# A kernel that orders its own instructions: new durations in the estimate behind the order

## The chip, the cores and the metric

The kernel runs on one core of a Trainium2 chip. The metric is device time in microseconds: the median of several executions of one build. The engines are TensorE (PE, with its weight loads PEld), VectorE (DVE), ScalarE (ACT), GpSimd (POOL) and SyncE (SP), which here only issues DMAs.

## The reference, cut to what matters

Two streams of 256 tokens, 1024 features each, pass two layers: stream 0 holds the latent tokens (h below), stream 1 the context (hc).

```python
def ffn_half_step(h, g, shift, scale, gate, w13, w2):
    return h + 0.5 * gate * swiglu(modulate(rms_norm(h, g), shift, scale), w13, w2)

def reference(x, c, ctx, c_ctx, w_ada, ...):
    h, hc = x, ctx
    for i in range(DEPTH):
        m = jnp.split((silu_c @ w_ada[i] + b_ada[i])[:, None, :], N_MOD, axis=-1)
        ...
        h = ffn_half_step(h, g_ffn1[i], m[0], m[1], m[2], w13_ffn1[i], w2_ffn1[i])
        hc = ffn_half_step(hc, g_ffn1[i], mc[0], mc[1], mc[2], w13_ffn1[i], w2_ffn1[i])
        n_lat = modulate(rms_norm(h, g_mix[i]), m[3], m[4])
        z = n_lat @ w_in[i]
        ...
        y = mix_heads(z, ...) @ w_out[i]
        h = h + m[5] * y
        h = ffn_half_step(h, g_ffn2[i], m[6], m[7], m[8], w13_ffn2[i], w2_ffn2[i])
        ...
    return rms_norm(h, g_final)
```

`mix_heads` is a Fourier mixer, a small attention, a gated mixer over chunks and a pooling mixer, side by side. In the last layer the context passes only the first half-step and the keys and values. The inner width of an FFN is 2816, in three parts of 8, 7 and 7 blocks of 128.

## The kernel before, in words

Features lie on the 128 partitions in eight channels, tokens along the free axis: 512 columns are both streams, 256 one of them. Every large product is made from three matmuls (`mm3`, lines 187 to 193): a weight tile of 128 x 1024 is loaded (tile stg), ScalarE rounds it (whi, line 156), VectorE takes the rest (wlo, line 164), and the activations are split in the same way (n, and ghi and glo inside an FFN). Five pairs whi and wlo are held; when a weight tile has been used (`done`), the next one is converted.

A normalisation at the end of a stage goes through these steps, for each stream: VectorE adds the last output to h (line 168), ScalarE squares it (sq, line 156), POOL adds the square to acc (line 464), two pairs of small matmuls against ones reduce acc (line 183), VectorE adds the epsilon (ss, line 173), POOL takes the power (rs, line 492), VectorE puts it on a diagonal (dg, line 164), a matmul broadcasts it, and `apply` makes for each channel nt (VectorE, line 168), the high part of n (ScalarE, line 156) and the low part of n (VectorE, line 168). The next stage's products begin with stream 0 (`gemm_start`): for each channel in turn the products of two weight tiles, then the same for two further tiles, and then stream 1. Meanwhile the last four outputs of the stage before were made for stream 0 first and for stream 1 after it (`final_half`), each with a product per inner block.

The order is not written out. While the program is built, the class `Weaver` keeps an estimated time: `W.t` for TensorE and `W.free` for the other engines. Each emitted instruction advances them by a cost. Tasks (a generator for each normalisation, conversion, evacuation, attention head and so on) say by `yield` at which estimated time they go on; after each product, `tick` runs those whose time has come, and what they emit stands in the queues at that place. Each engine then works through its queue in that order, and real waits come from semaphores alone. So a cost is never executed; it moves instructions past one another. A result counts as there 60 ns after its engine's estimated end:

```python
    def pe(self, cost, after=0.0):
        self.t = max(self.t, after) + cost
        end = self.t + 150.0
        self.tick()
        return end

    def on(self, engine, cost, after=0.0):
        start = max(self.free[engine], after, self.t)
        self.free[engine] = start + cost
        return start + cost + 60.0
```

Where a product needs a channel whose n has not been emitted, `W.until` runs tasks ahead, in the order of their times, until it has; TensorE's estimated time then jumps. The costs touched are those of ScalarE (`act`, line 155), VectorE (`vcost`, line 160, and `vstt`, line 167), the products (`mm3`, line 187; lines 1305 to 1308 and 1321 to 1324 in the mixing) and POOL (`square_in`, line 464, and `rstd_tail`, line 492). Loads are issued by SP from a fixed list (`loads`), each when the conversion that frees its buffer has been emitted.

Of the kernel before, what the change touches and what calls it, by code (L numbers as in the profile page):

```python
# [128 lines left out]
def block_kernel(ctx: ExitStack, tc: tile.TileContext, ins, out: bass.AP):  # L129
    nc = tc.nc  # L130
    W = Weaver()
# [23 lines left out]
    def act(o, i, func, after=0.0, n=None, **kw):  # L155
        nc.scalar.activation(o, i, func, **kw)  # L156
        n = n or int(np.prod(o.shape[1:]))
        return W.on("a", 190.0 + 0.833 * n, after)

    def vcost(o):  # L160
        return 70.0 + 1.04 * int(np.prod(o.shape[1:]))

    def vtt(o, a, b, op, after=0.0):
        nc.vector.tensor_tensor(out=o, in0=a, in1=b, op=op)  # L164
        return W.on("v", vcost(o), after)

    def vstt(o, a, s, b, op0, op1, after=0.0):
        nc.vector.scalar_tensor_tensor(out=o, in0=a, scalar=s, in1=b, op0=op0, op1=op1)  # L168
        return W.on("v", vcost(o), after)

    def vts(o, a, s1, op0, s2=None, op1=None, after=0.0):
        if op1 is None:
            nc.vector.tensor_scalar(out=o, in0=a, scalar1=s1, scalar2=None, op0=op0)
        else:
            nc.vector.tensor_scalar(out=o, in0=a, scalar1=s1, scalar2=s2, op0=op0, op1=op1)
        return W.on("v", vcost(o), after)
# [5 lines left out]
    def mm(o, l, r, first, last, after=0.0, skip=False):  # L182
        nc.tensor.matmul(o, l, r, start=first, stop=last, skip_group_check=skip)  # L183
        n = int(np.prod(r.shape[1:]))
        return W.pe(max(110.0, 1.68 * n), after)

    def mm3(o, wh, wl, xh, xl, first, last, after=0.0, skip=False):
        n = int(np.prod(xh.shape[1:]))
        c = max(109.0, 0.4235 * n)
        nc.tensor.matmul(o, wh, xh, start=first, stop=False, skip_group_check=skip)  # L190
        nc.tensor.matmul(o, wh, xl, start=False, stop=False, skip_group_check=skip)  # L191
        nc.tensor.matmul(o, wl, xh, start=False, stop=last, skip_group_check=skip)  # L192
        return W.pe(3 * c, after)
# [98 lines left out]
    def conv(i, j, hi, lo):  # L292
        n = loads[j][2]
        raw = stage[j][:, :n]
        yield act(hi[:, :n], raw, AF.Copy)
        ready_t[i] = vtt(lo[:, :n], raw, hi[:, :n].bitcast(F32), ALU.subtract)
        ready[i] = (hi[:, :n], lo[:, :n])
        use(j)
# [7 lines left out]
    def done(i):  # L306
        over.add(i)
        while finished[0] in over:
            i = finished[0]
            finished[0] += 1  # L310
            ready.pop(i)
            conv_upto(i + AHEAD)
# [60 lines left out]
    def gain_from(l, i, c0=0, c1=KC, n=2):  # L373

        m = mods[l][:, :n, (1, 4, 7)[i] * 8 + c0:(1, 4, 7)[i] * 8 + c1]
        vstt(gains[l][:, i, :n, c0:c1], m, 1.0,
             gains[l, "g"][:, i, None, c0:c1].to_broadcast([P, n, c1 - c0]), ALU.add, ALU.mult)
# [70 lines left out]
    def square_in(v, c):  # L448

        if v not in acc:  # L450
            acc[v] = tmp.tile([P, T], F32, name="acc%d" % v, tag="acc%d" % v, bufs=1)
            acc_n[v] = acc_i[v] = 0
        i = acc_i[v]
        acc_i[v] += 1
        if i == 0:
            t1 = act(acc[v], h[:, c, v], AF.Square)
        else:
            s = yield from SQ.get()
            t1 = act(s, h[:, c, v], AF.Square)
            if i == KC - 1 and last[0]:  # L460
                last_sq[v] = s
            else:
                yield t1
                nc.gpsimd.tensor_tensor(out=acc[v], in0=acc[v], in1=s, op=ALU.add)  # L464
                t1 = W.on("g", 640.0)
                SQ.put(s)
        acc_n[v] += 1
        acc_t[v] = t1
# [18 lines left out]
    def rstd_tail(ps, t1, nblk, n_feat):  # L487
        yield t1
        ss = tmp.tile([P, 4], F32, name="ss", tag="ss", bufs=8)
        t1 = vts(ss[:, :nblk], ps[:, :nblk], n_feat * EPS, ALU.add, after=t1)  # L490
        rs = tmp.tile([P, 4], F32, name="rs", tag="rs", bufs=8)
        nc.gpsimd.tensor_tensor(out=rs[:, :nblk], in0=ss[:, :nblk], in1=mhalf.to_broadcast([P, nblk]), op=ALU.pow)
        t1 = W.on("g", 380 + 165 * nblk, t1)
        yield t1
        dg = yield from DG.get()
        dv = dg[:, :P * nblk].rearrange("p (b q) -> p b q", b=nblk)
        t1 = vtt(dv, ident[:, None, :].to_broadcast([P, nblk, P]),
                 rs[:, :nblk, None].to_broadcast([P, nblk, P]), ALU.mult, t1)
        yield t1
        t1 = mm(ps[:, :P * nblk], ones, dg[:, :P * nblk], True, True, t1)  # L500
        DG.put(dg)
        yield t1
# [6 lines left out]
    def n_of(c, v):  # L509
        if v is None:  # L510
            a = nt_[c][:, :4 * T].rearrange("p (v x) -> p v x", v=2)
            return a[:, :, :T], a[:, :, T:]
        o = 2 * T * v
        return nt_[c][:, o:o + T], nt_[c][:, o + T:o + 2 * T]
# [16 lines left out]
    def raw_in(l, i, c):  # L531
        hi, lo = (t[:, :T] for t in raw_of(c))
        x, a = h[:, c, 0], gain_of(l, i, 0, c)
        yield act(hi, x, AF.Copy, scale=a)
        vstt(lo, x, a, hi.bitcast(F32), ALU.mult, ALU.subtract)
        raw_done.add(c)
# [36 lines left out]
    def wk(i, k, n=P):  # L573
        a, b = get(i)
        return a[:, k * n:(k + 1) * n], b[:, k * n:(k + 1) * n]

    def ps_new():
        W.until(lambda: MM.free)
        return MM.take()
# [5 lines left out]
    def gemm(i, vs, nk=KC, xs=None, ps=None, ok=None, raw=False):  # L585

        ps = ps or ps_new()
        v = None if len(vs) == 2 else vs[0]
        o = ps[:, :T + 2] if raw else cols(ps, vs)
        for k in range(nk):  # L590
            wh, wl = wk(i, k)
            if ok:
                W.until(lambda: ok(k))
            xh, xl = raw_of(k) if raw else (xs or n_of)(k, v)
            mm3(o, wh, wl, xh, xl, k == 0, k == nk - 1)
        return ps
# [332 lines left out]
    def mixing(l, tail):  # L929
# [4 lines left out]
        with ExitStack() as es:  # L934
# [350 lines left out]
            def ev(o, i, f, key):  # L1285
                t1 = act(o, i, f) if f else vcopy(o, i)
                MM.put(key[1])
                yield t1
                st[key[0]] += 1
# [9 lines left out]
            for b in blks:  # L1299
                ps = ps_new()  # L1300
                v, tk = b // 2, slice((b % 2) * P, (b % 2) * P + P)
                for kk in range(KC):
                    wh, wl = wk(i0 + 5 + kk // 4, kk % 4, T)
                    xh, xl = n_of(kk, v)
                    nc.tensor.matmul(ps[:, :T], xh[:, tk], wh, start=kk == 0, stop=False)  # L1305
                    nc.tensor.matmul(ps[:, :T], xh[:, tk], wl, start=False, stop=False)  # L1306
                    nc.tensor.matmul(ps[:, :T], xl[:, tk], wh, start=False, stop=kk == KC - 1)
                    W.pe(327.0)
                W.spawn(ev(vg[:, b], ps[:, :T], AF.Gelu_apprx_tanh, ("vg", ps)), W.t + 200.0)
            done(i0 + 5)  # L1310
            done(i0 + 6)
            for v in vs:
                pss = [ps_new() for _ in range(2)]
                halves_ = ((0,), (1,)) if v != vs[-1] else ((0, 1),)
                for bs_ in halves_:
                    for kk in range(KC):
                        wh, wl = wk(i0 + 7 + kk // 2, kk % 2, 512)
                        xh, xl = n_of(kk, v)
                        for b in bs_:
                            ps, tk = pss[b], slice(b * P, b * P + P)  # L1320
                            nc.tensor.matmul(ps, xh[:, tk], wh, start=kk == 0, stop=False)  # L1321
                            nc.tensor.matmul(ps, xh[:, tk], wl, start=False, stop=False)  # L1322
                            nc.tensor.matmul(ps, xl[:, tk], wh, start=False, stop=kk == KC - 1)  # L1323
                            W.pe(648.0)
                        if kk % 2 and v == vs[-1]:
                            done(i0 + 7 + kk // 2)
                    for b in bs_:
                        W.spawn(ev(FP[:, 2 * v + b], pss[b], None if b else AF.Copy, ("fp", pss[b])), W.t + 200.0)
                n_free.add(v)
# [35 lines left out]
    vts(gfin, gfin, 32.0, ALU.mult)  # L1365
    begin_mods(1)
    mixing(0, norm_next(0, 2))
    load_pk2(1)
    ffn(0, 2, [0, 1], norm_next(1, 0))
# [140 lines left out]
```

## Time and profile before

| | us |
|---|---|
| median of 3 runs (1602.47 to 1604.53) | 1602.86 |
| the profiled execution's own time | 1602.9 |
| its span, from the first to the last instruction | 1600.8 |
| TensorE busy in the span | 1569.0 |
| VectorE, ScalarE, POOL busy | 1016.2, 559.3, 94.8 |

Times in rows count from the start of the span. The span is read against the profiled execution's own time: 2.1 us lie around it. TensorE's matmuls are pipelined, so the recorded duration of one overlaps with the next one's; its pace is read from how many start in a stretch. Inside an FFN half-step the kernel streams weight tiles; the boundaries where one stage's normalisation leads into the next stage's products are at about 390, 555, 920 and 1290 us, the mixings at 412 to 555 and 1310 to 1400 us.

### The profile page before, as it was taken

The numbers are of one execution on the slowest core, as the hardware profiler recorded it, in microseconds if no ns is written. First come the engines' busy times: TensorE is split into PE (matmuls) and PEld (weight loads), VectorE is DVE, ScalarE is ACT, GpSimd is POOL, SyncE is SP. The second block draws the span as 40 slices with busy tenths as digits, with TensorE's granted clock in tenths as the row PEclk, the third lists the DMA queues.
The fourth block names the chain that finished last, engine by engine and source line by source line (L and its number), as shares of the span: only waits on it lengthen the run. The fifth ranks groups of instructions, "written<-read, shape, count | busy, mean of one in ns | idle before, by whom it ended". The sixth has DMA issues, their size and how long they took to land.

```text
span 1600.8 us, 22427 instructions
## 1 busy us (share of the span) xinstructions
PE 1569.0 (98%) x8868; PEld 1348.3 (84%) x8868; DVE 1016.2 (63%) x1718; ACT 559.3 (35%) x845; POOL 94.8 (6%) x93
## 2 busy tenths in 40 slices
PE   6999999999999999999999999999999999999997
PEld 4788888889967998888888898888888897899997
DVE  5478787878657466555563366786563367776674
ACT  3332231323435352223222243222222355554443
POOL 0000000004100310000000210000000121100001
PEclk9999999999999999999999999999999999999999
DMA  9456655664211144354352234566473223265551
GB/s 354 191 168 206 196 190 179 221 193 154 80 38 53 55 183 163 122 170 137 129 171 93 77 113 164 176 236 231 160 237 111 93 86 106 92 204 180 167 193 61
DMA packets 72056, 245.52 MB, mean 153 GB/s; under 512 B 8336, under 2 KB 10640, under 8 KB 71184
## 3 DMA queue, kind: packets, MB, share of 16 engines
q1 hardware_dynamic: 71664, 243.71, 45.0%
q8 instruction: 69, 1.13, 0.3%
q10 hardware_dynamic: 288, 0.39, 0.1%
q14 instruction: 35, 0.29, 0.1%
HBM read 243.03 MB, written 1.05 MB: 152 GB/s over the span
## 4 chain that ended last, share of the span: by engine, by line
PE 94%; DVE 3%; ACT 1%; issue 1%; POOL 0%; DMA 0%; SPq 0%; DVEq 0%; ACTq 0%; POOLq 0%
PE mm L191 28%; PE mm L190 28%; PE mm L192 28%; PE mm L183 5%; DVE wlo L164 1%; PE mm L1321 1%; PE mm L1323 1%; PE mm L1322 1%; PE mm L196 1%; DVE nt L168 1%; DVE n L168 1%; PE mm L400 1%; POOL acc L464 0%; PE mm L1305 0%; PE mm L1306 0%
## 5 line engine op out<-in xcount | busy, mean ns | idle before, releaser
L190 PE MATMUL mm<-n,whi 128*128 128x512 f32 (+2 forms) x1804 | 624.4, 346 | 3.1 <-ACT whi L156 3.1
L191 PE MATMUL mm<-n,whi 128*128 128x512 f32 (+2 forms) x1804 | 620.4, 344 | 4.1 <-DVE n L168 3.3
L192 PE MATMUL mm<-n,wlo 128*128 128x512 f32 (+2 forms) x1804 | 617.8, 342 | 0.5 <-DVE wlo L164 0.5
L156 ACT ACTIVATE whi<-stg 128x1024 fp32r<-128x1024 f32 (+1 forms) x310 | 318.2, 1032 | 447.8 <-PE mm L191 194.1
L164 DVE TENSOR_TENSOR wlo<-stg,whi 128x1024 fp32r<-128x1024 f32 (+1 forms) x310 | 374.5, 1211 | 92.8 <-ACT whi L156 92.5
L190 PEld LDWEIGHTS mm<-n,whi 128*128 128x128 f32 x1804 | 343.4, 190 | 46.6 <-issue 4.8
L191 PEld LDWEIGHTS mm<-n,whi 128*128 128x128 f32 x1804 | 343.2, 190 | 46.7 <-DVE n L168 6.9
L192 PEld LDWEIGHTS mm<-n,wlo 128*128 128x128 f32 x1804 | 343.7, 191 | 39.5 <-DVE wlo L164 1.0
L426 DVE SCALAR_TENSOR_TENSOR junk<-stg,sbc 128x1024 bf16<-128x1024 f32 x224 | 274.5, 1226 | 8.1 <-DMA stg<-in_w_ada 6.1
L190 PE MATMUL mm<-ghi,whi 128*128 128x512 f32 (+1 forms) x788 | 270.8, 344 | 0.0
L191 PE MATMUL mm<-glo,whi 128*128 128x512 f32 (+1 forms) x788 | 270.2, 343 | 0.0
L192 PE MATMUL mm<-ghi,wlo 128*128 128x512 f32 (+1 forms) x788 | 270.0, 343 | 0.0
L168 DVE SCALAR_TENSOR_TENSOR h<-mm,gates,h 128x256 f32<-128x256 f32 x168 | 75.6, 479 | 147.0 <-PE mm L192 146.8
L191 PEld LDWEIGHTS mm<-glo,whi 128*128 128x128 f32 x788 | 149.3, 189 | 17.7
L190 PEld LDWEIGHTS mm<-ghi,whi 128*128 128x128 f32 x788 | 149.3, 189 | 17.4
L192 PEld LDWEIGHTS mm<-ghi,wlo 128*128 128x128 f32 x788 | 149.3, 189 | 17.3
L464 POOL TENSOR_TENSOR acc<-acc,sq 128x256 f32<-128x256 f32 x68 | 71.2, 1054 | 1361.1 <-ACT sq L156 1184.6
L164 DVE TENSOR_TENSOR g<-mm,s 128x512 f32<-128x512 f32 x66 | 45.6, 691 | 167.1 <-PE mm L192 166.5
L156 ACT ACTIVATE ghi<-g 128x512 fp32r<-128x512 f32 (+1 forms) x88 | 50.9, 578 | 275.4 <-DVE g L164 261.8
L164 DVE TENSOR_TENSOR glo<-g,ghi 128x512 fp32r<-128x512 f32 (+1 forms) x88 | 54.5, 620 | 18.2 <-ACT ghi L156 18.2
L156 ACT ACTIVATE n<-nt,mods 128x256 fp32r<-128x256 f32 x80 | 39.7, 508 | 69.5 <-DVE nt L168 68.6
L156 ACT ACTIVATE sq<-h 128x256 f32<-128x256 f32 x70 | 28.6, 416 | 86.3 <-DVE h L168 86.1
(151 smaller groups left out, 798.0 us busy)
## 6 DMA issues: line engine op xcount, KB each, us to landing
stg<-in_w_ffn SPq DMA_DIRECT2D x208, 512.0 KB, 4.2
stg<-in_w_ada SPq DMA_DIRECT2D x128, 512.0 KB, 3.8
stg<-in_w_ffn SPq DMA_DIRECT2D x64, 448.0 KB, 3.1
stg<-in_w_in SPq DMA_DIRECT2D x22, 512.0 KB, 3.3
stg<-in_w_out SPq DMA_DIRECT2D x16, 512.0 KB, 3.3
sbc<-in_cb SPq DMA_DIRECT2D x3, 1024.0 KB, 7.0
pk<-in_pk SPq DMA_DIRECT2D x2, 1344.0 KB, 8.3
h<-in_xT SPq DMA_DIRECT2D x4, 512.0 KB, 6.0
```

Of the source, the lines that this page charges most:

```text
L156: nc.scalar.activation(o, i, func, **kw)
L164: nc.vector.tensor_tensor(out=o, in0=a, in1=b, op=op)
L168: nc.vector.scalar_tensor_tensor(out=o, in0=a, scalar=s, in1=b, op0=op0, op1=op1)
L183: nc.tensor.matmul(o, l, r, start=first, stop=last, skip_group_check=skip)
L190: nc.tensor.matmul(o, wh, xh, start=first, stop=False, skip_group_check=skip)
L191: nc.tensor.matmul(o, wh, xl, start=False, stop=False, skip_group_check=skip)
L192: nc.tensor.matmul(o, wl, xh, start=False, stop=last, skip_group_check=skip)
L196: nc.tensor.transpose(o, i, ident)
L400: nc.tensor.matmul(ps[32 * g:32 * g + 32, :P], sc[:, k], w[:, 128 * g:128 * g + 128], start=k == 0, stop=k == KC - 1)
L426: nc.vector.scalar_tensor_tensor(out=ada_tiles["junk"], in0=stage[j], scalar=1.0, in1=ada_tiles["s"][:, v], op0=ALU.mult, op1=ALU.mult, ac ...
L464: nc.gpsimd.tensor_tensor(out=acc[v], in0=acc[v], in1=s, op=ALU.add)
L1321: nc.tensor.matmul(ps, xh[:, tk], wh, start=kk == 0, stop=False)
```

## The change

Only numbers of the estimate change. ScalarE: 200 + 0.834 ns per element in place of 190 + 0.833, or 280 where a bias or a scale goes in. VectorE: 150 + 1.045 ns per element in place of 70 + 1.04, and 60 more for an instruction with three operands. A matmul of a product: 118 ns up to 258 columns and 0.4434 ns per column above, in place of 109 or 0.4235. POOL: 1050 in place of 640 for the sum, 300 + 330 per block in place of 380 + 165 for the power. The three matmuls of the mixing's transposed products: 354 in place of 327 and 681 in place of 648.

```diff
@@ -155,10 +155,10 @@
     def act(o, i, func, after=0.0, n=None, **kw):
         nc.scalar.activation(o, i, func, **kw)
         n = n or int(np.prod(o.shape[1:]))
-        return W.on("a", 190.0 + 0.833 * n, after)
+        return W.on("a", (280.0 if "bias" in kw or "scale" in kw else 200.0) + 0.834 * n, after)
 
     def vcost(o):
-        return 70.0 + 1.04 * int(np.prod(o.shape[1:]))
+        return 150.0 + 1.045 * int(np.prod(o.shape[1:]))
@@ -166,7 +166,7 @@
     def vstt(o, a, s, b, op0, op1, after=0.0):
         nc.vector.scalar_tensor_tensor(out=o, in0=a, scalar=s, in1=b, op0=op0, op1=op1)
-        return W.on("v", vcost(o), after)
+        return W.on("v", vcost(o) + 60.0, after)
@@ -186,7 +186,7 @@
     def mm3(o, wh, wl, xh, xl, first, last, after=0.0, skip=False):
         n = int(np.prod(xh.shape[1:]))
-        c = max(109.0, 0.4235 * n)
+        c = 118.0 if n <= 258 else 0.4434 * n
@@ -462,7 +462,7 @@
                 nc.gpsimd.tensor_tensor(out=acc[v], in0=acc[v], in1=s, op=ALU.add)
-                t1 = W.on("g", 640.0)
+                t1 = W.on("g", 1050.0)
@@ -490,7 +490,7 @@
         nc.gpsimd.tensor_tensor(out=rs[:, :nblk], in0=ss[:, :nblk], in1=mhalf.to_broadcast([P, nblk]), op=ALU.pow)
-        t1 = W.on("g", 380 + 165 * nblk, t1)
+        t1 = W.on("g", 300 + 330 * nblk, t1)
@@ -1305,7 +1305,7 @@
-                    W.pe(327.0)
+                    W.pe(354.0)
@@ -1321,7 +1321,7 @@
-                            W.pe(648.0)
+                            W.pe(681.0)
```

## Rows read from the trace of the kernel before

**Rows 1.** The page: busy time by engine, and the chain that ended last by engine.
```profile
PE 1569.0 (98%) x8868; PEld 1348.3 (84%) x8868; DVE 1016.2 (63%) x1718; ACT 559.3 (35%) x845; POOL 94.8 (6%) x93
...
PE 94%; DVE 3%; ACT 1%; issue 1%; POOL 0%; DMA 0%; SPq 0%; DVEq 0%; ACTq 0%; POOLq 0%
```

**Rows 2.** Busy time in five stretches: from:to, us, busy by engine, clock, DMA, GB/s.
```profile
390.00:412.00 22.00, 19.75 (x129) 18.27 (x128) 17.80 (x40) 9.96 (x18) 7.27 (x6) 0.84 0.29 96
555.00:575.00 20.00, 19.04 (x154) 18.51 (x153) 16.77 (x33) 9.31 (x17) 6.34 (x6) 1.00 0.47 176
920.00:945.00 25.00, 23.09 (x168) 21.72 (x167) 20.35 (x42) 12.66 (x23) 7.85 (x7) 0.93 0.25 85
1290.00:1310.00 20.00, 17.67 (x131) 16.16 (x132) 17.83 (x37) 10.98 (x19) 5.98 (x6) 1.00 0.32 106
1310.00:1400.00 90.00, 88.53 (x599) 73.90 (x598) 67.42 (x136) 51.68 (x108) 10.86 (x9) 1.00 0.29 98
```

**Rows 3.** The same view of two steady stretches inside FFN half-steps.
```profile
80.00:120.00 40.00, 40.00 (x178) 33.11 (x177) 30.38 (x44) 12.81 (x18) 0.00 (x0) 1.00 0.52 168
1440.00:1480.00 40.00, 40.00 (x334) 40.00 (x334) 25.20 (x39) 16.73 (x20) 0.00 (x0) 1.00 0.54 184
```

**Rows 4.** Waits of TensorE: us in total, times, longest us.
```profile
PE mm L183 <- POOL acc L464: 3.4, 4, 0.9
PE mm L191 <- DVE n L168: 3.3, 7, 0.7
...
PE mm L183 <- DVE es L164: 2.1, 2, 1.6
```

**Rows 5.** Groups of instructions by form: busy us, mean ns of one, idle before.
```profile
L164 DVE TENSOR_TENSOR wlo<-stg,whi 128x1024 fp32r<-128x1024 f32 x246 | 304.2, 1240 | 75.0 <-ACT whi L156 74.8
...
L464 POOL TENSOR_TENSOR acc<-acc,sq 128x256 f32<-128x256 f32 x68 | 71.2, 1054 | 1361.1 <-ACT sq L156 1184.6 <-issue 173.4 <-ACT n L156 2.9
```

**Rows 6.** VectorE's timeline at the first boundary: start us, duration us, instruction.
```profile
400.52 0.47 DVE L168 SCALAR_TENSOR_TENSOR h<-mm,gates,h 128x256 f32<-128x256 f32 x1
400.91 0.47 DVE L168 SCALAR_TENSOR_TENSOR n<-nt,mods,n 128x256 fp32r<-128x256 f32 x1
401.31 1.21 DVE L164 TENSOR_TENSOR wlo<-stg,whi 128x1024 fp32r<-128x1024 f32 x1
402.44 0.47 DVE L168 SCALAR_TENSOR_TENSOR nt<-h,gains,mm 128x256 f32<-128x256 f32 x1
```

**Rows 7.** POOL's timeline there, idle time before and its releaser in brackets.
```profile
388.45 0.74 POOL L464 TENSOR_TENSOR acc<-acc,sq 128x256 f32<-128x256 f32 x1 [1.78 <-ACT sq L156]
...
401.64 1.46 POOL L464 TENSOR_TENSOR acc<-acc,sq 128x256 f32<-128x256 f32 x1 [2.08 <-ACT sq L156]
```

**Rows 8.** TensorE's timeline: the reduction for stream 1 at 403 and 569 us.
```profile
403.16 0.92 PE L183 MATMUL mm<-ones,acc 128*128 128x1 f32 x4 [0.86 <-POOL acc L464]
...
569.58 0.61 PE L183 MATMUL mm<-ones,acc 128*128 128x1 f32 x4 [0.86 <-POOL acc L464]
```

**Rows 9.** VectorE's timeline at 934 us: the fourth channel's n, and ss.
```profile
934.05 0.55 DVE L168 SCALAR_TENSOR_TENSOR n<-nt,mods,n 128x256 fp32r<-128x256 f32 x1
935.02 0.16 DVE L173 TENSOR_SCALAR ss<-mm 128x2 f32<-128x2 f32 x1 [0.41 <-PE mm L183]
```

**Rows 10.** VectorE's timeline at 555 to 575 us: the fourth n, the last h.
```profile
565.67 0.96 DVE L168 SCALAR_TENSOR_TENSOR n<-nt,mods,n 128x256 fp32r<-128x256 f32 x1
...
566.96 0.46 DVE L168 SCALAR_TENSOR_TENSOR h<-mm,mods,h 128x256 f32<-128x256 f32 x1
```

**Rows 11.** Busy time and granted clock in three stretches after the reductions.
```profile
403.20:410.00 6.80, 6.58 (x26) 5.94 (x27) 4.10 (x11) 2.17 (x5) 0.88 (x1) 0.51 0.24 77
...
935.60:939.10 3.50, 3.41 (x17) 3.10 (x15) 2.27 (x6) 1.53 (x3) 0.36 (x1) 0.52 0.20 81
...
1303.80:1309.00 5.20, 4.81 (x35) 4.14 (x34) 4.61 (x13) 2.96 (x6) 0.48 (x1) 1.00 0.16 65
```

## The prediction

> **What bounds the kernel now.** I read the page first: TensorE is busy for 98% of the span and holds 94% of the chain that ended last [rows 1]. A new order of the same instructions can therefore win only what TensorE loses by waiting or by a low clock. The table of stretches tells where that is [rows 2, 3]: inside an FFN half-step TensorE is busy all the time; what is missing lies in the second mixing (1.5 of 90 us idle) and at four boundaries where a normalisation ends a stage: idle 2.3 us at 390, 1.0 us at 555, 1.9 us at 920 and 2.3 us at 1290. The waits name the cause [rows 4]: the reduction of the squares waits four times for POOL's last sum, 3.4 us in all, and products wait seven times for n, the low part of a channel from VectorE, 3.3 us. So the boundaries can give back at most about 7.5 us of idle time, and what the clock adds to that (below).
>
> **The pace of TensorE.** In steady stretches 178 matmuls of 512 columns pass in 40 us, or 334 of about 256 [rows 3]: 225 and 120 ns each. The new 227 and 118 say this; the old 217 and 109 were 4% and 9% too low. The products themselves stay as they are and cost nothing more: only their place in the estimate's time moves.
>
> **The pace of the other engines.** The new figures are the rows' durations: 1220 ns against 1240 for wlo, 1050 against 1054 for POOL's sum [rows 5], 477 ns against 0.47 us for h and nt [rows 6]. But the starts in a row show something else [rows 6]: h starts at 400.52 us, n at 400.91, wlo at 401.31, nt at 402.44. The next instruction starts 0.39 us after one that is recorded with 0.47, and 1.13 us after a wlo that is recorded with 1.21: VectorE is occupied for 0.08 us less than the duration. The old 1135 ns for wlo was nearer to this, the old 336 ns for h and nt 0.05 us short, the new 477 is 0.09 us long. The Trainium skill, page Perfetto Trace Analysis, section Optimizing Scalar/DVE Operations, speaks against the change in the same way: an instruction's profiled latency is longer than the engine's busy time, since the acknowledgement of the write overlaps with the next instruction. The trace agrees [rows 6]; by that rule alone the VectorE edits bring nothing, and the sum below would be 0.
>
> POOL's sum is not one number either: 0.74 us at 388.45, 1.46 us at 401.64 while wlo runs [rows 6, 7]. 1050 lies between the two; the last sum of a boundary, which TensorE waits for, is the long one. The Trainium skill, page SBUF — State Buffer, section SBUF: two separate sides, has the rule: GpSimd and a VectorE instruction with two SBUF inputs exclude each other for a whole instruction. The trace agrees with it [rows 6, 7]; by it no constant fits both cases. The remaining edits (ScalarE with a bias, rs, the mixing's products) move the estimate the same way and are in the counts that follow.
>
> **The change at a boundary, step by step.** A tick of the estimate is one product of three matmuls: 327 ns before, 354 after. From stream 0's last product on, the estimate has the update of h at tick 1, the square at 3, the sum at 5, and the reduction is due at 1635 + 640 + 60 = 2335 ns before and 1770 + 1050 + 60 = 2880 after: tick 8 before, 9 after, so one product (0.36 us) later. Then ss, rs and dg: with all costs put in, the broadcast matmul stays at tick 16 at the boundaries that an FFN ends, and goes from 14 to 16 at 555 us; a wlo holds VectorE there meanwhile, so I cost that at nothing (0.2 us if that cover is gone).
>
> Then the channels. `apply` resumes 336 + 60 - 100 = 296 ns after nt before, which is one tick, and after 300 ns more, one tick: a channel every 2 ticks (0.72 us of TensorE). After, 477 + 60 - 100 = 437 ns is over 354: two ticks, and then one: a channel every 3 ticks (1.08 us). VectorE itself needs 2 x 0.39 = 0.79 us. Stream 1's last four outputs take seven ticks each, and a weight tile and an h go with each: before, 2289 = 1135 + 336 + 672c gives c = 1.2 channels; after, 2478 = 1220 + 477 + 954c gives 0.8; the chip can do (2.52 - 1.13 - 0.39) / 0.79 = 1.3. Followed tick by tick, VectorE's order at 390, 920 and 1290 us stays the same up to the second channel's n. Then stream 1's last h goes ahead of the fourth nt, and the fourth tile's wlo, now behind the third n (401.31 after 400.91 [rows 6]), goes ahead of it. No wait is added, and no DMA changes its place: SP issues the loads from a fixed list.
>
> The bill, boundary by boundary:
> - At 390 us the third n starts 1.13 us later, about 402.05, and its two products end about 403.2. h and the square come 0.39 us earlier, so the sum is ready by then. Before, the reduction started at 403.16, after waiting [rows 8]. Cost 0.1 us: the wait moves from the sum to n.
> - At 920 and 1290 us it is the same, but there the fourth n stood ahead of ss (934.05 and 935.02 [rows 9]); now it stands behind, starts about 935.1 in place of 934.05 and is late for products that could start about 935.1 and need it complete (0.47 us): 0.4 us each.
> - At 555 us an output takes eight ticks, and four n were through before the last h (565.67 and 566.96 [rows 10]). With 3 ticks a channel two are through, and the fourth wlo stands ahead of the fourth n. Five channels' products ended with the reduction waiting 0.9 us until 569.58 [rows 8], so they began about 569.6 - 0.9 - 5 x 0.72 = 565.1. From there h, n, nt, wlo end at 565.1 + 3 x 0.39 + 1.13 = 567.4 at best, the fourth n with its 0.47 and the wait for whi about 568.2, when three channels' products have been over for 1 us; the fifth n stands behind ss and costs 0.6 us more (an estimate from the 0.92 and 0.61 us of the reductions, which ss waits for [rows 8]). That is 1.6 in place of 0.9: 0.7 us.
>
> Bounds where the trace has no such row: the second mixing and the start. There the other engines' figures grow together with TensorE's, and new waits cannot be read. The idle time there, 1.5 us in the mixing and 2.1 us for es at the start [rows 2, 4], is the most to be gained; I take the same amounts as the most to be lost, and the middle, 0, because neither end is nearer to a row. At the tail each step waits for the one before, whatever the estimate: 0.
>
> Sum: 0.1 + 0.7 + 0.4 + 0.4 = 1.6 us on the profiled execution's own 1602.9 us, which agrees with the median of the runs shown (1602.86): **1604.5 us**. About 0.2% (3.2 us) can be told from no change here, so the forecast is no change.
>
> **Rivals.** (A) Faster: the truer pace of TensorE and POOL puts the reductions behind ready sums, and the clock stays up. For it: there are four such waits [rows 4], and a low clock follows two of them, granted 0.51 (1.2 GHz instead of 2.4) from 403.2 to 410 and 0.52 from 935.6 to 939.1, while 1303.8 to 1309 had 1.00 [rows 11]. At the latter's rate 26 matmuls take 26/35 x 5.2 = 3.9 us, not 6.8, and 17 take 2.5, not 3.5: 3.9 us lost. With half of the 3.4 us this gives 1602.9 - 5.6 = 1597.3 us. Against it: VectorE is the engine that is late, and it does no less. Chance 0.23.
>
> (B) Slower: the clock falls at the other two boundaries as well. Before, a wait of TensorE at a boundary was at most 0.9 us long [rows 4]; with wlo ahead of the third n there is one of 1.5 to 2 us. It decides as soon as such a wait lowers the clock at 555 and 1290 us, which have 1.00 now [rows 2]. Price: the 1.6 us and twice the mean of 2.9 and 1.0 us: 1602.9 + 1.6 + 3.9 = 1608.4 us. Against it: at 1290 us 2.3 us of idle time left the clock at 1.00. Chance 0.30.
>
> (C) The change does not do what it says: all figures grow by similar shares, and what moves is hidden: 1602.9 us. For it: until the second n my count gives the very same order. Against it: 3 ticks in place of 2. Chance 0.17.
>
> **Numbers.** The forecast has 0.30; it and C are no change, 0.47; faster 0.23; slower 0.30. The forecast's own range is 1602.9 to 1606. From 1597 (A) to 1609 (B) some 0.18 is left out, stronger forms of A and B; the unknown 3.6 us of mixing and start lie inside.
>
> **What would show it.** Right: wlo ahead of the third n on VectorE near 401, 932 and 1301 us; waits for POOL's sum near 0 in the list, waits for n of 5 us or more; 178 and 334 matmuls in 40 us as before. A: the waits for n fall too, and no stretch has 0.5. B: a third and a fourth stretch at 0.5. Wrong altogether: a wait inside an FFN half-step, or a mixing longer by over 2 us; I foresee neither.

## The result and the profile after

The changed kernel takes 1622.14 us (median of four runs, 1621.01 to 1623.26) against 1603.55 for the kernel before (four runs, 1602.47 to 1604.53): a ratio of 1.0118, interval 1.0105 to 1.0130. It is slower by 18.6 us, where 1604.5 us and no change had been forecast; the forecast's own range ended at 1606 and that with the rivals at 1609. The profiled execution took 1621.01 us; its span is 1619.1 us, 18.3 more than before.

The page of the kernel after, busy time by engine and the chain by engine [rows 1]:

```profile
PE 1574.0 (97%) x8880; PEld 1352.0 (83%) x8880; DVE 1019.4 (63%) x1718; ACT 557.8 (34%) x845; POOL 97.1 (6%) x93
...
PE 93%; DVE 4%; issue 1%; ACT 1%; POOL 0%; DMA 0%; SPq 0%; DVEq 0%; ACTq 0%; POOLq 0%
```

The work is the same; VectorE still does 1718 instructions. Of the 18.3 us, 13.3 are idle time of TensorE (45.1 us in place of 31.8); the other 5.0 are more busy time, of which the lower clock told below is a part. The waits of TensorE after, in us in total, times and longest [rows 4], say what it waited for:

```profile
PE mm L191 <- DVE n L168: 10.4, 11, 2.2
PE mm L192 <- DVE wlo L164: 9.5, 4, 3.2
...
PE mm L183 <- POOL acc L464: 0.9, 1, 0.9
```

The wait for POOL's sum has shrunk as predicted, from 3.4 to 0.9 us (the one that is left is at the boundary of 555 us), and the wait for n has grown from 3.3 to 10.4. Products also wait 9.5 us for wlo, the low part of a weight tile. The same line before:

```profile
PE mm L192 <- DVE wlo L164: 0.5, 1, 0.5
```

Of the 9.5 us, 2.0 are at the start and 7.5, in three waits, inside the first FFN half-step. Steady stretches show it: one of before, then three of after (the table of stretches, columns as in [rows 2, 3]):

```profile
240.00:280.00 40.00, 40.00 (x178) 33.13 (x177) 31.65 (x55) 7.46 (x9) 0.00 (x0) 1.00 0.54 181
```

```profile
80.00:120.00 40.00, 40.00 (x178) 33.13 (x177) 29.51 (x42) 12.94 (x17) 0.00 (x0) 1.00 0.51 172
240.00:280.00 40.00, 37.34 (x165) 30.61 (x164) 29.83 (x50) 7.20 (x9) 0.00 (x0) 1.00 0.54 176
360.00:400.00 40.00, 35.19 (x194) 30.47 (x194) 26.47 (x41) 11.46 (x20) 12.26 (x10) 0.96 0.48 162
```

The first stretch after has the 178 matmuls of [rows 3]. The next two lie inside the first FFN half-step and lack 2.7 and 4.8 us of TensorE at a granted clock of 1.00 and 0.96: the place that the prediction had left out as full.

**A ledger by stage.** I divided both spans at the first weight load for a product on n or on ghi of each part and took the differences of the stage lengths. Every part of the other FFN half-steps is the same to 0.01 us, apart from the stretches where a half-step ends.

| stage | us more after |
|---|---|
| start, and the first part's first matrix | 0.9 |
| first half-step, 2nd matrix of the second part (243.5 to 281.6 before) | 2.95 |
| first half-step, last part (281.6 to 398.1 before) | 0.2 + 7.3 |
| from there through the first mixing to 655 us | 2.4 |
| end of the second half-step and boundary at 930 us | 0.35 + 1.05 |
| end of the third half-step, boundary at 1298 us and second mixing | 0.35 + 2.8 |
| sum | 18.3 |

So 10.5 us are lost in the first half-step, some 7 at the boundaries, 0.9 at the start. Each kernel has one trace, and over the traces of all runs below the start lies between 1.5 us less and 1.7 us more than before: its 0.9 us mean little.

**The first half-step.** There VectorE also takes the sums that make the modulation vectors out of w_ada (tile junk, line 426), two for each tile of w_ada. VectorE's timeline before, one period:

```profile
267.76 0.88 DVE L168 SCALAR_TENSOR_TENSOR h<-mm,gates,h 128x256 f32<-128x256 f32 x2 [0.60 <-PE mm L192]
268.56 1.22 DVE L426 SCALAR_TENSOR_TENSOR junk<-stg,sbc 128x1024 bf16<-128x1024 f32 x1
...
269.70 1.09 DVE L164 TENSOR_TENSOR wlo<-stg,whi 128x896 fp32r<-128x896 f32 x1
270.70 1.22 DVE L426 SCALAR_TENSOR_TENSOR junk<-stg,sbc 128x1024 bf16<-128x1024 f32 x1
```

Every 4.76 us come two h, a sum, wlo and a sum. The same timeline after:

```profile
268.69 0.88 DVE L168 SCALAR_TENSOR_TENSOR h<-mm,gates,h 128x256 f32<-128x256 f32 x2 [0.60 <-PE mm L192]
269.48 1.22 DVE L426 SCALAR_TENSOR_TENSOR junk<-stg,sbc 128x1024 bf16<-128x1024 f32 x1
...
270.74 1.22 DVE L426 SCALAR_TENSOR_TENSOR junk<-stg,sbc 128x1024 bf16<-128x1024 f32 x1
...
273.45 0.88 DVE L168 SCALAR_TENSOR_TENSOR h<-mm,gates,h 128x256 f32<-128x256 f32 x2 [1.47 <-PE mm L192]
274.24 1.22 DVE L426 SCALAR_TENSOR_TENSOR junk<-stg,sbc 128x1024 bf16<-128x1024 f32 x1
...
275.38 1.09 DVE L164 TENSOR_TENSOR wlo<-stg,whi 128x896 fp32r<-128x896 f32 x1
```

One period has no wlo: it comes behind the next h, which itself waits 1.47 us for TensorE. Its data were not late. Of the eight tiles of 896 columns in this part it is the seventh, and the seventh load and the seventh whi came long before it, as SP's and ScalarE's timelines after show:

```profile
262.30 0.33 SPq L262 DMA_DIRECT2D stg<-in_w_ffn  x1
```

```profile
266.66 0.95 ACT L156 ACTIVATE whi<-stg 128x896 fp32r<-128x896 f32 x1 [3.17 <-DMA stg<-in_w_ffn]
```

TensorE's timeline after has the first two matmuls of that product, which need whi alone, and the third, which waits for wlo:

```profile
273.25 0.39 PE L190 MATMUL mm<-ghi,whi 128*128 128x512 f32 x1
273.48 0.39 PE L191 MATMUL mm<-glo,whi 128*128 128x512 f32 x1
276.52 0.50 PE L192 MATMUL mm<-ghi,wlo 128*128 128x512 f32 x1 [2.66 <-DVE wlo L164]
```

whi was there from 267.61 us on. What held wlo until 275.38 was its place in VectorE's queue: behind two sums (269.48, 270.74), the h of 273.45 and a third sum. So TensorE stood still for 2.66 us. The same happens twice more, with waits of 3.18 us until 380.16 and 1.63 us until 393.27; there the loads had landed 5.8 and 6.7 us before whi began, and whi too stood late in its queue.

The plan put these conversions late, and the kernel's code says by which way. The sums have a gate, line 424: a sum is put off while VectorE is booked for over 300 ns beyond TensorE's estimated time (`while W.free["v"] > W.t + 300.0`). Loads go in a fixed order through five buffers, and in the plan a load counts as issued only when the load five places ahead of it on the list has been used; its conversion gets its estimated time from there (`arrival`, line 263). Tiles of w_ada, which are not converted, stand between the weight tiles on that list and count as used when their last sum is emitted. So a sum that is put off moves the conversions behind it to a later place in the queues, whatever the chip does. When the changed kernel is built, `get` (line 300) finds four tiles of the first half-step not yet converted as TensorE's estimated time reaches them, and three of them are those that TensorE waited for; in the kernel before and in those of runs 1, 3, 4 and 9 below it finds none there. That is worked out from the code; that the gate makes the loss is shown on the chip by run 3.

**The boundaries.** The four boundaries in the table of stretches after, each moved by what the span had grown until there, so that it answers to a line of [rows 2], and the second mixing:

```profile
401.40:423.40 22.00, 18.59 (x120) 17.23 (x119) 17.32 (x37) 9.36 (x17) 6.16 (x6) 0.84 0.26 96
567.50:587.50 20.00, 18.05 (x139) 16.87 (x139) 17.11 (x35) 9.87 (x18) 7.59 (x6) 1.00 0.47 176
934.20:959.20 25.00, 21.78 (x156) 20.39 (x155) 20.18 (x41) 11.78 (x22) 7.69 (x7) 0.93 0.25 85
1305.60:1325.60 20.00, 16.01 (x110) 14.75 (x109) 16.37 (x33) 8.89 (x17) 6.15 (x6) 0.91 0.31 106
1325.60:1415.60 90.00, 88.30 (x594) 73.61 (x593) 67.77 (x137) 52.44 (x108) 12.55 (x9) 1.00 0.28 94
```

Idle time of TensorE is 3.4, 1.95, 3.2 and 4.0 us where it was 2.3, 1.0, 1.9 and 2.3: 1.1, 1.0, 1.3 and 1.7 more. The mixing has 1.7 us in place of 1.5. VectorE's timeline after, at the first boundary, has the predicted order:

```profile
412.03 0.47 DVE L168 SCALAR_TENSOR_TENSOR nt<-h,gains,mm 128x256 f32<-128x256 f32 x1
412.42 1.21 DVE L164 TENSOR_TENSOR wlo<-stg,whi 128x1024 fp32r<-128x1024 f32 x1
413.55 0.94 DVE L168 SCALAR_TENSOR_TENSOR n<-nt,mods,n 128x256 fp32r<-128x256 f32 x1
```

wlo is ahead of the third n (at 920 and 1290 us too), and TensorE's timeline shows a wait of 2.16 us in place of 0.56 us for the third n and 0.86 us for the sum [rows 8]:

```profile
414.54 0.39 PE L191 MATMUL mm<-n,whi 128*128 128x256 f32 x1 [2.16 <-DVE n L168]
```

Lastly the clock: four stretches at about half (1.2 GHz) after, where there were two [rows 11] (both kernels have one more in their tail, the last 6 us of the span, left out here):

```profile
380.70:384.10 3.40, 3.40 (x10) 2.65 (x9) 3.10 (x4) 0.00 (x0) 0.00 (x0) 0.54 0.47 150
414.90:421.70 6.80, 6.58 (x30) 6.00 (x28) 3.73 (x10) 2.28 (x5) 0.88 (x1) 0.51 0.16 64
950.70:954.10 3.40, 3.40 (x18) 3.22 (x17) 2.15 (x6) 1.16 (x3) 0.13 (x1) 0.54 0.00 0
1319.40:1322.80 3.40, 2.98 (x13) 2.78 (x14) 2.46 (x7) 1.02 (x2) 0.88 (x1) 0.53 0.13 53
```

Those at 414.9 and 950.7 answer to the two of before; those at 380.7 and 1319.4 are new, behind long waits of TensorE (3.18 us until 380.16, 2.01 us until 1318.18).

### The profile page after: what moved, and what is told of

Same layout as the page of the kernel before. It is cut to its first block, busy times and chain, and to the rows that moved or that the text cites. A ratio compares the mean times of both kernels' runs of the same rounds, so it can differ in the third digit from the quotient of the medians.

```text
span 1619.1 us, 22446 instructions
## 1 busy us (share of the span) xinstructions
PE 1574.0 (97%) x8880; PEld 1352.0 (83%) x8880; DVE 1019.4 (63%) x1718; ACT 557.8 (34%) x845; POOL 97.1 (6%) x93
## 3 DMA queue, kind: packets, MB, share of 16 engines
HBM read 243.03 MB, written 1.05 MB: 151 GB/s over the span
## 4 chain that ended last, share of the span: by engine, by line
PE 93%; DVE 4%; issue 1%; ACT 1%; POOL 0%; DMA 0%; SPq 0%; DVEq 0%; ACTq 0%; POOLq 0%
PE mm L191 28%; PE mm L190 28%; PE mm L192 28%; PE mm L183 5%; DVE wlo L164 1%; PE mm L1321 1%; PE mm L400 1%; PE mm L1323 1%; PE mm L1322 1%; DVE n L168 1%; PE mm L196 1%; DVE nt L168 0%; DMA sbc<-in_w_ada 0%; POOL rs L492 0%; PE mm L1305 0%
## 5 line engine op out<-in xcount | busy, mean ns | idle before, releaser
L191 PE MATMUL mm<-n,whi 128*128 128x512 f32 (+2 forms) x1808 | 622.4, 344 | 11.7 <-DVE n L168 10.4
```

## The experiments

The theories. **Load**: the new figures make the estimate's VectorE fuller than the real one; the gate puts off the sums of w_ada, buffers come free late in the plan, and wlo is late in the first half-step. **Late vector**: at the boundaries the truer, longer steps put n behind other work of VectorE, and the wait moves from the sum to n. **Ticks**: that happens because a channel takes three products of the estimate in place of two. **Occupation**: the harm at both places is that the estimate holds VectorE for the whole recorded duration, and not that results count as ready later. Each kernel computes the whole reference; only numbers of the estimate differ. Each ratio is to executions of the kernel before taken beside it (medians 1603.2 to 1603.9 us).

**1. VectorE's old figures in the changed kernel (v_old).**

```diff
-        return 150.0 + 1.045 * int(np.prod(o.shape[1:]))
+        return 70.0 + 1.04 * int(np.prod(o.shape[1:]))
-        return W.on("v", vcost(o) + 60.0, after)
+        return W.on("v", vcost(o), after)
```

> The changed kernel with VectorE's figures as before (70 + 1.04 per element, nothing more for three operands); TensorE, ScalarE and POOL keep the new ones. Theory Load (the estimate makes VectorE too busy: in the products of the second FFN matrix two h, two sums for the modulation and one wlo are 954 + 2524 + 1086 = 4564 of 4767 ns, 96%, where before it was 4198 of 4553, 92%, and so wlo falls behind the next h): the 9.5 us of waits for wlo in the first half-step vanish, 1600 to 1607 us. Rival Pace (TensorE's slower figures move the conversions against the products): these waits stay, 1613 us or more.

Measured: 1606.26 us (1605.32 to 1607.96), 1.0018 of before, interval 1.0009 to 1.0028. The first half-step is as before to 0.4 us, the wait for wlo 0.5 us, so the loss there hangs on VectorE's figures. The waits for n do not: they stay nearly as long as after.

```profile
PE mm L191 <- DVE n L168: 9.7, 7, 1.5
```

By the division of the ledger the boundaries and mixings still lose 2.9 us in place of 6.9. Run 10, with POOL's figures taken back as well, has 3.7 us of waits for n and loses nothing there.

**2. VectorE's 150 + 1.045 n alone, in the kernel before (v_half).**

```diff
-        return 70.0 + 1.04 * int(np.prod(o.shape[1:]))
+        return 150.0 + 1.045 * int(np.prod(o.shape[1:]))
```

> The kernel before with VectorE's 150 + 1.045 per element alone; nothing more for three operands, TensorE, ScalarE and POOL as before. Load: 834 + 2524 + 1086 = 4444 of 4553 ns, 98%, is more than the changed kernel has, so waits for wlo in the first half-step of 8 us or more, and 1612 us or more. Pace: TensorE's figures are the old ones, so no such waits, 1600 to 1607 us.

Measured: 1622.92 us (1620.63 to 1623.9), 1.0119 (1.0104 to 1.0134): one line brings the whole loss. Two stretches of the first half-step grow, by 4.7 and 8.4 us (the first part's second matrix and the last part's), and the waits of TensorE in this kernel show the same two names:

```profile
PE mm L192 <- DVE wlo L164: 7.3, 4, 2.8
PE mm L191 <- DVE n L168: 6.9, 14, 1.2
```

**3. The changed kernel with a wider gate (gate).**

```diff
-            while W.free["v"] > W.t + 300.0:
+            while W.free["v"] > W.t + 1500.0:
```

> The changed kernel, all figures new; only the condition under which a sum for the modulation is put off is loosened: VectorE has to be estimated 1500 ns behind in place of 300. Load, by way of this gate (a sum put off frees its staging buffer late, the next weight load waits for the buffer, and its conversion falls behind h): the waits for wlo in the first half-step shrink to under 3 us, the boundaries keep theirs, 1609 to 1615 us. If the gate is not the link, the waits stay and it is 1619 to 1625 us.

Measured: 1609.86 us (1609.62 to 1612.35), 1.0043 (1.0028 to 1.0058), 12 us less than after. The first half-step is as before to 0.4 us, which is 10 of the 12; some 2 lie at the start. The boundaries keep their loss. The waits of TensorE in this kernel:

```profile
PE mm L191 <- DVE n L168: 10.9, 12, 2.2
...
PE mm L192 <- DVE wlo L164: 2.0, 1, 2.0
```

The wait of 2.0 us for wlo is at the start; in the half-step there is none. All figures of the change are there, and the 10.5 us of the half-step are gone but for 0.4: the gate is the link between figure and loss.

**4. The estimate tells occupation from duration (split).** An engine is held for the distance of starts that the trace shows, and its result counts as there later.

```diff
-        return start + cost + 60.0
+        return start + cost + tail + 60.0
-        return W.on("a", (280.0 if "bias" in kw or "scale" in kw else 200.0) + 0.834 * n, after)
+        return W.on("a", (180.0 if "bias" in kw or "scale" in kw else 100.0) + 0.834 * n, after, 100.0)
-        return 150.0 + 1.045 * int(np.prod(o.shape[1:]))
+        return 70.0 + 1.04 * int(np.prod(o.shape[1:]))
-        return W.on("v", vcost(o) + 60.0, after)
+        return W.on("v", vcost(o) + 56.0, after, 80.0)
```

(`on` takes `tail` as a further argument, 0 where none is given. VectorE's other instructions have the tail of 80 too.)

> The changed kernel with the recorded duration split in two: VectorE and ScalarE are taken as occupied for the distance from one start to the next (70 + 1.04 per element, 56 more for three operands; ScalarE 100, or 180 with bias or scale, + 0.834), and the result as ready 80 and 100 ns after that. Load: VectorE is 2 x 392 + 2524 + 1002 = 4310 of 4767 ns, 90%, so no waits for wlo in the first half-step and boundaries near those of before: 1598 to 1606 us. If late results and not occupation do the harm, the waits stay: 1613 us or more.

Measured: 1604.47 us (1603.89 to 1607.61), 1.0010 (1.0001 to 1.0019). Both losses go. VectorE is held for the old figure again, with 56 ns more for three operands, and its results still count as late.

**5. TensorE's figures alone, in the kernel before (pe_only).**

```diff
-        c = max(109.0, 0.4235 * n)
+        c = 118.0 if n <= 258 else 0.4434 * n
-                    W.pe(327.0)
+                    W.pe(354.0)
-                            W.pe(648.0)
+                            W.pe(681.0)
```

> The kernel before with TensorE's figures alone (118 or 0.4434 per column, 354, 681). Load: VectorE is 4198 of 4767 ns, 88%, in the products of the second matrix, so no wait for wlo in the first half-step. Theory Late vector (at the boundaries VectorE is late whatever the estimate says): the total stays within 3 us of before, 1600 to 1606 us. Rival A of the prediction (a truer pace of TensorE puts the reductions behind ready sums): waits for POOL's sum under 1 us, at most one stretch at half clock, 1599 us or less.

Measured: 1598.48 us (1597.82 to 1599.95), 0.9970 (0.9959 to 0.9981). This part is a gain of some 5 us; by stages, 3.5 us between 398 and 655 us and 2.3 at the boundary of 930 us. But the reductions still wait for POOL's sum, as the waits of TensorE in this kernel show:

```profile
PE mm L183 <- POOL acc L464: 3.1, 4, 0.9
...
PE mm L191 <- DVE n L168: 1.5, 4, 0.6
```

The waits for n fell (3.3 before), and one stretch at half clock is left. So the time came out as Rival A had it, but not by its way.

**6. POOL's figures alone (pool_only).**

```diff
-                t1 = W.on("g", 640.0)
+                t1 = W.on("g", 1050.0)
-        t1 = W.on("g", 380 + 165 * nblk, t1)
+        t1 = W.on("g", 300 + 330 * nblk, t1)
```

> The kernel before with POOL's figures alone (1050 for the sum, 300 + 330 per block for the power). The reduction at a boundary moves by about one product of 0.36 us. Late vector: the waits for POOL's sum shrink from 3.4 to about 2 us and return as waits for n; 1601 to 1606 us. Rival A: what they shrink by is gained, 1600 us or less.

Measured: 1605.12 us (1603.28 to 1607.36), 1.0011 (1.0002 to 1.0020). The waits of TensorE in this kernel, with those of [rows 4] beside them:

```profile
PE mm L191 <- DVE n L168: 6.6, 9, 1.5
...
PE mm L183 <- POOL acc L464: 0.9, 1, 0.9
```

2.5 us of wait for the sum went and 3.3 us of wait for n came. So POOL's figures alone make this trade of waits.

**7. The changed kernel without the 60 ns for three operands (stt_old).**

```diff
-        return W.on("v", vcost(o) + 60.0, after)
+        return W.on("v", vcost(o), after)
```

> The changed kernel without the 60 ns for three operands (h and nt 417 in place of 477); all else new. Load: 834 + 2524 + 1086 = 4444 of 4767 ns, 93%, stands between 92% (no wait for wlo) and 96% (9.5 us of them): waits for wlo of 0 to 5 us in the first half-step, 1605 to 1615 us. If the 60 ns matter only at the boundaries and the 80 ns for every instruction do the harm in the half-step, its waits stay at 9 us, 1617 to 1623 us.

Measured: 1618.79 us (1617.28 to 1620.65), 1.0100 (1.0085 to 1.0116). The first half-step loses the same 10.5 us, so the 80 ns on each instruction suffice. At 390 us wlo stands behind the third n again, and by the division of the ledger the boundaries and mixings lose 4.1 us in place of 6.9: the 60 ns have their part there. The share of a period that the estimate gives VectorE does not set the size of the loss as I had thought. One period has two h, two sums of 1262 and one wlo against seven products: before (2 x 336 + 2 x 1262 + 1002) / 4553 = 92.2%, no loss; here 4444 / 4767 = 93.2%, the whole loss; after 4564 / 4767 = 95.7%, the same loss. The real share is 88%: in the timeline before, the starts stand 0.80, 1.14 and 1.00 us apart, and the last sum ends 1.23 us after its start: 4.17 of 4.76. Whether the share or the gate's 300 ns against one instruction's length decides stays open.

**8. The wide gate, and a channel back at two products (pace).**

```diff
-            while W.free["v"] > W.t + 300.0:
+            while W.free["v"] > W.t + 1500.0:
-                yield t1 - 100.0
+                yield t1 - 200.0
```

> The kernel called gate with one more edit: between nt and n of a channel the estimate resumes 200 ns ahead of nt's estimated end in place of 100, so 337 in place of 437 ns and one tick in place of two: a channel every 2 ticks as before, at the new figures. Theory Ticks (three ticks a channel put wlo ahead of the third n): the three boundary stretches, 2.0 + 2.3 + 2.8 us longer than before in gate, lose half of that or more, 1602 to 1607 us. If the mixings or the later reductions make these us, they stay: 1608 to 1612 us.

Measured: 1610.93 us (1610.90 to 1613.21), 1.0053 (1.0040 to 1.0066), no better than gate, and wlo still stands ahead of the third n at 390, 920 and 1290 us. Ticks falls: the moment at which `apply` resumes isn't what orders the boundaries.

**9. VectorE held as long as before, its results 80 or 140 ns later (v_tail).** In the changed kernel, with the argument `tail` of run 4 (the last pair of lines stands in three places):

```diff
-        return 150.0 + 1.045 * int(np.prod(o.shape[1:]))
+        return 70.0 + 1.04 * int(np.prod(o.shape[1:]))
-        return W.on("v", vcost(o) + 60.0, after)
+        return W.on("v", vcost(o), after, 140.0)
-        return W.on("v", vcost(o), after)
+        return W.on("v", vcost(o), after, 80.0)
```

> The changed kernel with VectorE's new figures kept for when a result is ready (80 ns later, 140 for three operands) and the old ones for how long the engine is taken; TensorE, ScalarE and POOL stay new. Occupation (the overestimated occupation of VectorE does the harm): no wait for wlo over 2 us in the first half-step, its two stretches of the second matrix within 1 us of before, total 1601 to 1609 us. Readiness (results estimated later put the conversions later): the 10.5 us of these stretches stay, 1615 us or more.

Measured: 1604.06 us (1602.98 to 1605.00), 1.0002 (0.9992 to 1.0011). Each result counts as ready at the same distance from its start as in the changed kernel, to 5 ns; only the time that VectorE is held differs, and that is worth 18 us. Occupation holds, at the boundaries too: VectorE's timeline of this kernel has wlo behind the third n again, in the order of [rows 6].

```profile
400.97 0.47 DVE L168 SCALAR_TENSOR_TENSOR n<-nt,mods,n 128x256 fp32r<-128x256 f32 x1
401.37 1.21 DVE L164 TENSOR_TENSOR wlo<-stg,whi 128x1024 fp32r<-128x1024 f32 x1
402.50 0.47 DVE L168 SCALAR_TENSOR_TENSOR nt<-h,gains,mm 128x256 f32<-128x256 f32 x1
```

**10. TensorE's and ScalarE's figures, without VectorE's and POOL's (pe_act).** It is v_old with the two lines of POOL as before the change.

```diff
-                t1 = W.on("g", 1050.0)
+                t1 = W.on("g", 640.0)
-        t1 = W.on("g", 300 + 330 * nblk, t1)
+        t1 = W.on("g", 380 + 165 * nblk, t1)
```

> The kernel before with TensorE's and ScalarE's new figures; VectorE and POOL as before. With TensorE's alone it was 1598.5 us, with POOL's as well as these two 1606.3. If POOL's figures lose the difference (a later reduction at each boundary): 1596 to 1601 us. If ScalarE's do (80 to 90 ns more for each n puts it behind): 1603 us or more.

Measured: 1596.35 us (1595.02 to 1597.98), 0.9953 (0.9941 to 0.9966): the fastest of all, 7 us under the kernel before. Which change of order gains it was not followed. Its boundaries in the table of stretches:

```profile
555.00:575.00 20.00, 19.50 (x156) 18.86 (x155) 17.92 (x38) 10.55 (x20) 4.89 (x5) 1.00 0.48 175
915.00:940.00 25.00, 23.93 (x189) 22.93 (x188) 19.74 (x40) 12.16 (x22) 6.97 (x8) 1.00 0.26 85
1285.00:1310.00 25.00, 23.29 (x188) 22.56 (x187) 23.41 (x47) 17.24 (x34) 6.50 (x6) 1.00 0.39 127
```

Idle 0.5, 1.1 and 1.7 us, and the clock stays at 1.00 in all three.

**11 and 12. POOL's old figures in split and in v_tail (split_pool_old, v_tail_pool_old).** The edit is that of run 10, made in those kernels.

> The kernel called split with POOL's figures as before. If POOL's figures cost at the boundaries in every company, it gains on split (1604.5): 1597 to 1602 us. If they cost only beside the old VectorE figures, it stays at 1603 to 1606 us.

> The kernel called v_tail with POOL's figures as before: TensorE and ScalarE new, VectorE taken as long as before with results 80 or 140 ns later. If POOL's figures cost the same in this company as between v_old (1606.3) and pe_act (1596.4): 1592 to 1597 us, at or below pe_act. If the later results of VectorE already move the reductions, POOL's figures cost little here: 1599 to 1604 us.

Measured: 1600.23 us (1598.02 to 1601.84), 0.9975 (0.9965 to 0.9985), and 1606.78 us (1603.14 to 1608.51), 1.0018 (1.0009 to 1.0027). With the new POOL figures split is 4.2 us slower, v_old 9.9 us slower than pe_act, but v_tail is 2.7 us faster. The last answer fits neither expectation. A part of it may be the clock, in three stretches of v_tail_pool_old:

```profile
403.10:409.90 6.80, 6.58 (x31) 6.11 (x30) 3.95 (x11) 2.11 (x5) 0.88 (x1) 0.52 0.17 67
935.60:939.00 3.40, 2.98 (x13) 2.82 (x13) 2.44 (x7) 1.02 (x2) 0.88 (x1) 0.53 0.27 106
1304.20:1307.60 3.40, 3.30 (x14) 3.12 (x15) 1.96 (x6) 1.02 (x2) 0.61 (x1) 0.53 0.03 11
```

That is 13.6 us at half clock, and v_tail has one stretch of 3.4. By the prediction's two prices (2.9 us for 6.8 and 1.0 for 3.4) the 10.2 us between them are worth some 3 to 4.4 us, more than the 2.7. That is an estimate from one execution of each, no proof: what POOL's figures do depends on what stands beside them, and why stays open. A kernel with TensorE's figures and the wide gate (pe_gate) has no time, so what the gate costs without VectorE's long figures stays open too.

## Why the prediction was wrong

**The step that failed** is the one on VectorE's occupation. The prediction read from the starts that VectorE is held 0.08 us less than the record says [rows 6], and then costed the overestimate at the four boundaries alone. Of a wait inside an FFN half-step it said that it foresaw none, since TensorE is busy there all the time [rows 3]. But a full TensorE is a result of the order, not a reserve. The row of 80 to 120 us, with VectorE busy 30.4 of 40 us, spoke of a stretch that indeed stayed full; of the tighter one from 243 us on no row was read, and one of the table would hardly have told (31.65 of 40 us): what counts is the period of 4.76 us, in which VectorE is held for 88%. And the step from a wrong load to what uses the load, the gate on line 424, was never made: the costs were followed as places in a queue at the boundaries alone. Its "no DMA changes its place" holds for the list of loads and not for the conversions that the estimate times by that list. Runs 1, 3 and 9 show cause and effect: without the long occupation, or with a wide gate, the 10.5 us are gone. The way between is read from the code and from the order in the queues.

**The longer record.** The Trainium skill, page Perfetto Trace Analysis, section Optimizing Scalar/DVE Operations, says that the write acknowledgement overlaps with the next instruction, and the trace agrees (starts 0.39 us apart at a recorded 0.47). The prediction drew from it that by that rule alone the VectorE edits bring nothing. That was the wrong conclusion from a right rule: a planner that is told the longer figure holds work back. Experiment 9 separates the two and finds 18 us between them.

**The boundaries**: the order was foreseen rightly, its reason and its size were not. wlo stands ahead of the third n, the waits merge, that for the sum nearly goes (3.4 to 0.9) and that for n comes (3.3 to 10.4; 5 or more was foreseen). The bill was 0.1, 0.7, 0.4 and 0.4 us; idle time grew by 1.1, 1.0, 1.3 and 1.7. Only at 555 us was it near. At 390 us TensorE waited 0.60, 0.56 and 0.86 us before (for two n and the sum) and 0.68 and 2.16 after, 0.8 more where 0.1 had been billed: the third n itself takes 0.94 us beside the POOL sum of 412.75, where the prediction had its recorded 0.47. The reason given for the order, three ticks a channel in place of two, fell with run 8; VectorE's estimated occupation makes it (run 9). The waits for n have a second source, POOL's figures (runs 1, 6 and 10).

**The mixing and the start**, costed at 0 within 1.5 and 2.1 us: idle time in the mixing grew by 0.2, and the start by 0.9, within what it differs by from trace to trace. That held; the 2.8 us of its stage are mostly the boundary ahead of it.

**Rival A** (faster) was half right. The truer pace of TensorE is worth some 5 us and with ScalarE's figures 7 us (runs 5 and 10), and the clock does stay up (one stretch of 3.4 us). But the reductions get behind ready sums in part only (3.1 us of wait in run 5, 1.3 in run 10), and the VectorE and POOL edits that come with it undo it. **Rival B** (slower by the clock) came true in part: two more stretches at half clock, one at the 1290 boundary as it said and one in the first half-step, where it had none; at 555 us, its other place, the clock stayed at 1.00. By the prediction's price of 1.0 us for such a stretch they are worth some 2 of the 18 us, an estimate. **Rival C** fell.

## What to carry to other kernels

In a planner, give each instruction two numbers: how long it holds its engine (the distance between starts in a dense stretch) and when its result is there (the recorded duration). Feeding the record into the first made this plan worse with truer-looking numbers. Two numbers took that loss away, and no more: split is no faster than the kernel before, and pe_act, with VectorE's and POOL's old figures, is 8 us faster than split. A truer estimate is not by itself a faster order. Before you change costs, look for every place where the estimate is a condition (a gate, a backlog limit, a buffer's release), and work out the estimated load of the stage with the least slack, not of a typical one; then change the figures of one engine at a time, since here TensorE's and ScalarE's gained 7 us and VectorE's lost 16 to 20 (runs 1, 2 and 9).

## What the runs showed of the hardware that was not expected

VectorE stood idle with ready work in its queue: from 271.97 to 273.45 us after, it waited 1.47 us for the h at the head of the queue, while the wlo of 275.38 had had its input since 267.61, and TensorE then waited 2.66 us for that wlo. The half-clock stretches didn't follow the idle time of their boundary alone: before, 1.9 us idle at 920 us went with one and 2.3 us at 1290 us with none [rows 2, 11]. And POOL's sum again had two lengths after the change, 0.73 us at 409.14 and 1.45 us at 412.75, begun behind the wlo of 412.42. In the first case the wlo that began behind it was the long one, 1.76 us in place of the 1.21 of 412.42. POOL's and VectorE's timelines after:

```profile
409.14 0.73 POOL L464 TENSOR_TENSOR acc<-acc,sq 128x256 f32<-128x256 f32 x1 [2.52 <-ACT sq L156]
412.75 1.45 POOL L464 TENSOR_TENSOR acc<-acc,sq 128x256 f32<-128x256 f32 x1 [2.88 <-ACT sq L156]
```

```profile
409.19 1.76 DVE L164 TENSOR_TENSOR wlo<-stg,whi 128x1024 fp32r<-128x1024 f32 x1
```

One constant, 640 or 1050 for the sum or 1220 for wlo, is wrong for one of the two cases.
